# Moving 30 loads from SyncE's to GpSimd's DMA queue, new places for the input's accumulations, and other buffer counts, in an encoder layer of two sequences

## The chip, the cores and the metric

The kernel runs on one core of a Trainium2 chip. The metric is the device time in microseconds (us) of one execution. Names in the text: TensorE (PE in the profile), VectorE (DVE), ScalarE (ACT), GpSimd (POOL) and SyncE (SP). "SPq" and "POOLq" in the profile are the instruction streams of SP and GpSimd that issue transfers. Each engine works through its own instructions strictly in order; a wait at the head of one holds all that stands behind it.

## The reference

One layer of an encoder is applied to two sequences of 1024 rows and 1024 columns, each with its own conditioning vector c:

```python
def layer(x, c, ...):
    mod = jax.nn.silu(c) @ w_ada + b_ada
    sh1, sc1, ga1, sh2, sc2, ga2 = [m[:, None, :] for m in jnp.split(mod, N_MOD, axis=-1)]
    h = rmsnorm(x, g_mix) * (1.0 + sc1) + sh1
    z = h @ w_in
    q_lat, kv_lat, k_pe, f_in = ...                       # 256, 128, 64, 512 columns
    y_mla = mla_group(q_lat, kv_lat, k_pe, ...)           # attention, 4 heads, softmax over 1024 keys
    y_four = fourier_group(f_in, w_four)                  # 2-D Fourier mixing, real part
    mix = jnp.concatenate([y_mla, y_four], axis=-1) @ w_out
    x = x + ga1 * mix
    h2 = rmsnorm(x, g_ffn) * (1.0 + sc2) + sh2
    ffn = (jax.nn.silu(h2 @ w_gate) * (h2 @ w_up)) @ w_down
    return x + ga2 * ffn
```

In the attention, w_uq expands the normalised q_lat to the queries, of which 64 columns per head are rotated (rope); the keys are never expanded, since w_ukv's key part is absorbed into the queries. All arithmetic is float32; a float32 operand is split into a high part and a remainder (`split`), and a product is made of three matmuls (`mm3`, lines 83 to 85 of the profile).

## The kernel before, in words

Four stages follow each other in the profiled execution: the input projection and the Fourier transform up to about 230 us, the Fourier part's output up to about 305, the attention up to about 764, and then the feed-forward network (FFN), whose products are made by sub-block combinations with fewer multiplications (seven sums H of blocks of the normalised rows). The change concerns the third stage and its border to the fourth. Arrays named `..._d` lie in DRAM.

The attention is cut into 64 items k = 0 to 63, `items`: sequence s, block b of 256 rows, head h, half u of 128 rows. i = k % 8 is an item's place in its block. The code of the loop gives the order in which an item's work is written down, a scheduler puts each engine's instructions in order from that, and `tc.issue_after` adds constraints. What an item does:

- `scores`: TensorE makes 128 x 1024 scores (L1191 to L1200) from the absorbed queries qa and the rotated ones qp; VectorE takes the maximum mx and nb (L1206, L1207), ScalarE the exponential, VectorE 1/sum, rr, and scales p by it (L1210, L1211). SP then copies p to pr by DMA, 512 KB (`pr<-p`, L1213). pr has two buffers, so item k's copy can start once item k−2 has been transposed.
- `flip_p`, two items later: TensorE transposes pr (`ppt<-identr,pr`, L1227), ScalarE and VectorE split the result into pt; `values` multiplies pt with the latent values (`gb<-pt,ckv`) into o0b, o1b.
- the queries of the next block: `rope_q` at i = 3, 4 (through the tile hv, named qt: L847 on VectorE, L848 on GpSimd, L852 qsk), `rope_flip` at i = 5, 6 (`pqt`, L858), `absorb_q` after each odd item (qa).
- the block before: `out_step` loads its rows of the sum so far (`x<-fo_d`, L1120), adds the projection of the attention's result (`out_proj`, L1130; its bank is `gb`, of which there are two), stores them to x_d (`norm2`, L1135), normalises them (squares on ScalarE L1138, `rstd` on GpSimd L107 to L114, xn on VectorE L1143) and stores them transposed to h_d (`flip_h`, L1162).

Further work is hung on chosen items by the lists `todo[k]`:

- `add_x(i)`, 16 times: GpSimd adds a 256 x 512 part of the input x to fo_d in DRAM by an accumulating DMA (`fo_d<-in_x_dram`, L806, 512 KB). fo_d holds the Fourier part's output already.
- `gate_half` and `wv_load` (items 0 and 2 for the first sequence, 34 and 37 for the second): the gate's half is loaded into gah (one buffer, L1246), the output weights wo_d into wvr in 4 parts of 256 KB each time (L1271), and GpSimd multiplies the two (L1272).
- `comb_h` (items 49, 51, 57, 59): loads two halves of 512 KB of the first sequence's normalised rows (`hca<-h_d`, L1252), GpSimd forms sums and differences hcb of them (L140, L143), the folded combinations for the FFN, and stores 1 MB (`hc_d<-hcb`, L1262). hca and hcb have one buffer each.

At the end of the attention the FFN's first data are fetched: `prep_h` loads the first sequence's H (L1368), the first weights rgu (L1378), and `x3_load` the last block's rows (x and X, L1401). VectorE and ScalarE split H (`H<-H,H`, L63) between the last projections; GpSimd's queue holds there the x_d stores of the last blocks (L1135).

Most of the transfers named stand on SP (`nc.sync.dma_start`); those of add_x, hc_d and the last x_d stores on GpSimd (`nc.gpsimd.dma_start`).

Of the kernel before, what the change touches and what calls it, by code (L numbers as in the profile page):

```python
# [12 lines left out]
F32 = mybir.dt.float32  # L13
F32R = mybir.dt.float32r
# [7 lines left out]
P = 128  # L22
# [3 lines left out]
HEADS = 4  # L26
# [26 lines left out]
def hybrid_encoder_kernel(ctx: ExitStack, tc: tile.TileContext, a: dict):  # L53
    nc = tc.nc
# [70 lines left out]
    wo_d = dram.tile([P, 4, D], F32, name="wo_d")  # L125
# [670 lines left out]
    S = {}  # L796
# [9 lines left out]
            nc.gpsimd.dma_start(fo_d[s][bs, gs], xs[s][bs, gs], accum_op=ALU.add)  # L806

    def half(name):
        return e.tile([P, 512], F32, tag="hv", name=name, bufs=1)

    def load_seq(s, lat):
        ckv = [e.tile([P, 8, KVL], F32R, tag=f"ckv{i}", name=f"ckv{i}", bufs=1) for i in range(2)]
# [16 lines left out]
        return e.tile([P, HEADS, P], F32R, tag="qp", name="qp", bufs=4)  # L829

    def qa_tiles():
        return [e.tile([P, 256], F32R, tag=f"qa{i}", name=f"qa{i}", bufs=2) for i in range(2)]

    def rope_q(s, b, u, bankf):
        ql = S["q", s, b]
# [339 lines left out]
    with ExitStack() as st:  # L1175
# [54 lines left out]
        def values(s, b, q):  # L1230
            ckv = S[s][1]
            pts = S.pop(("pt", s, b, q))
            if q == 0:
                S["o", s, b] = [tl.tile([P, HEADS, 256], F32R, tag=f"o{i}", name=f"o{i}b{s}{b}", bufs=3) for i in range(2)]
            o = [t[:, 2 * q : 2 * q + 2, :].rearrange("p h t -> p (h t)") for t in S["o", s, b]]
            po = gbank()
            for c in range(8):
                pth, ptl = (t[:, c % 4].rearrange("p i t -> p (i t)") for t in pts[c // 4])
                mm3(po, ckv[0][:, c, :], ckv[1][:, c, :], pth, ptl, c == 0, c == 7)
            split(o[0], o[1], po)  # L1240
# [7 lines left out]
        def comb_h(s, c):  # L1248
            A = e.tile([P, 4, 512], F32, tag="lat00", name="hca")
            B = e.tile([P, 4, 512], F32, tag="lat01", name="hcb")  # L1250
            for i in range(2):
                nc.sync.dma_start(A[:, 2 * i : 2 * i + 2, :], h2_d[s][:, c + 4 * i, :].rearrange("p (a b) -> p a b", a=2))  # L1252
            a11, a21, a12, a22 = (A[:, i, :] for i in range(4))
            with tc.issue_after(here["p"]):
                add(B[:, 0, :], a21, a22, nc.gpsimd)
                sub(B[:, 2, :], a11, a21, nc.gpsimd)

            def rest():
                with tc.issue_after(here["p"]):
                    sub(B[:, 1, :], B[:, 0, :], a11, nc.gpsimd)  # L1260
                    sub(B[:, 3, :], a12, B[:, 1, :], nc.gpsimd)
                    nc.gpsimd.dma_start(hc_d[s][:, c], B)  # L1262

            S["comb"] = rest

        def wv_load(s, g):
            gs = slice(512 * g, 512 * g + 512)
            raw4 = (w if s == 0 else e).tile([P, 4, 512], F32, tag=f"lat{1 - s}{g}", name="wvr4")
            for h in range(HEADS):
                raw = raw4[:, h, :]  # L1270
                nc.sync.dma_start(raw, wo_d[:, h, gs])  # L1271
                nc.gpsimd.tensor_tensor(out=raw, in0=raw, in1=S["ga"], op=ALU.mult)  # L1272
                S["wv", h, g] = raw

# [15 lines left out]
        for c, k in enumerate((49, 51, 57, 59)):  # L1290
            todo[k].append(lambda c=c: comb_h(0, c))
            todo[k + 1].append(lambda: S.pop("comb")())
        for i, k in enumerate((6, 8, 10, 12, 17, 18, 19, 25, 26, 27, 33, 34, 35, 41, 42, 43)):
            todo[k].append(lambda i=i: add_x(i))
        for u in range(2):
            todo[60 + u].append(lambda u=u: out_load(1, 2, u))
# [45 lines left out]
    with ExitStack() as st:  # L1342
# [10 lines left out]
        def prep_h(H, s, n):  # L1353
# [3 lines left out]
            def load(i):  # L1357
                k = HK[i]
                src = h2_d[s][:, HSRC[k][0] : HSRC[k][0] + 4, 512 * HSRC[k][1] : 512 * HSRC[k][1] + 512] \
                    if isinstance(HSRC[k], tuple) else hc_d[s][:, :, HSRC[k], :]  # L1360
                if HSTAGE[s][i] is None:
                    raw[k] = [val() for _ in range(4)]
                    for c in range(4):
                        nc.sync.dma_start(raw[k][c], src[:, c, :])
                else:
                    t = quad(HSTAGE[s][i])
                    for c in (0, 2):
                        nc.sync.dma_start(t[:, c : c + 2, :], src[:, c : c + 2, :])  # L1368
                    raw[k] = t

            ahead = 4 if s == 0 else 2
# [1 line left out]
            for i in range(ahead):  # L1373
                load(i)
                if s == 0 and i == 0:
                    S["rgu"] = w.tile([P, 2, 1024], F32, tag="X0", name="rgu0", bufs=1)
                    for j in range(2):
                        nc.sync.dma_start(S["rgu"][:, j, :], a["wgu"][j, 0])  # L1378
                    x3_load()
            if s == 0:  # L1380
                yield
# [14 lines left out]
        def x3_load():  # L1396
            X1 = quad("X1").rearrange("p a b -> p (a b)")
            for u in range(2):
                xn = X1[:, D * u : D * u + D]
                x2 = tl.tile([P, D], F32, tag="o0", name="x3", bufs=3) if u == 0 else xn  # L1400
                nc.sync.dma_start(x2, fo_d[1][(6 + u) * P : (7 + u) * P, :])  # L1401
                S["x2", 1, 3, u] = x2
                S["xn", 1, 3, u] = xn

# [70 lines left out]
        for n in range(4):  # L1475
# [1 line left out]
            if n == 1:  # L1477
                norm3(0)
            if n == 2:
                fw = [tl.tile([P, 2, 512], F32R, tag=f"o{i}", name=f"fw{i}", bufs=3) for i in range(2)]  # L1480
                for i in range(2):
                    split(fw[0][:, i, :], fw[1][:, i, :], w0[i])
            prep_step((2, 0, 1, 0)[n])
# [498 lines left out]
```

## Time and profile before

| | |
|---|---|
| median of 3 runs | 2049.7 us (2049.03 to 2055.41) |
| profiled execution | 2048.47 us, span 2046.7 us |
| mean clock granted to TensorE | 0.989 |
| busy: TensorE, VectorE, ScalarE, GpSimd | 1984.9, 1425.1, 894.8, 829.5 us |
| DMA | 403.91 MB, mean 197 GB/s |
| SP's queue (q1) and GpSimd's (q0) | 344.27 MB and 57.81 MB |

A row of a timeline gives start, duration, engine, line, operation, tiles written and read, their count, and in brackets the time that the engine stood idle before, with what ended it. `x2` or `x3` behind a row means that equal instructions in succession were taken together, and its duration is then from the first one's start to the last one's end. A row of waits gives the microseconds in total, the number of waits and the longest. The duration of a DMA row is that of its issue, not of the transfer.

### The profile page before, as it was taken

How to read it: one execution, taken by the hardware profiler on the slowest of the kernel's cores; microseconds unless marked ns; L12 is line 12 of the kernel's file. 1: busy time of each engine (PE TensorE's matmuls, PEld its weight loads, DVE VectorE, ACT ScalarE, POOL GpSimd, SP SyncE). 2: the span in 40 equal slices, each digit the busy share in tenths (PEclk: the TensorE clock that was granted, in tenths of full speed). 3: DMA queues.
4: the chain of work that ended last, by engine and by line, in shares of the span. 5: the costliest groups of instructions: out<-in, count | busy, mean ns of one | idle time of the engine just before them, and what ended most of it. 6: DMA issues, size and time to landing. Idle time of an engine off the chain costs nothing.

```text
span 2046.7 us, 28591 instructions
## 1 busy us (share of the span) xinstructions
PE 1984.9 (97%) x9840; PEld 1620.8 (79%) x9840; DVE 1425.1 (70%) x2088; ACT 894.8 (44%) x1733; POOL 829.5 (41%) x1013
## 2 busy tenths in 40 slices
PE   8899998999999899999999999999999999999997
PEld 7688776788787777888888888877788888888876
DVE  5667757666677669888778676777765666667684
ACT  4565545455465455333333365453333333336441
POOL 2454122112213216888779510332664454420142
PEclk9999999999999899999999999999999999999999
DMA  9685795767675576546546587664332232258672
GB/s 377 203 292 172 253 338 180 205 175 207 207 189 189 193 285 211 200 161 221 182 152 221 170 286 251 218 235 157 125 123 103 92 114 104 94 188 279 221 232 88
DMA packets 191182, 403.91 MB, mean 197 GB/s; under 512 B 19580, under 2 KB 59260, under 8 KB 186940
## 3 DMA queue, kind: packets, MB, share of 16 engines
q1 hardware_dynamic: 172364, 344.27, 49.4%
q0 software_dynamic: 18672, 57.81, 9.5%
q8 instruction: 77, 1.26, 0.3%
q14 instruction: 69, 0.57, 0.1%
HBM read 256.46 MB, written 120.39 MB: 184 GB/s over the span
## 4 chain that ended last, share of the span: by engine, by line
PE 54%; DVE 3%; DMA 2%; POOL 1%; issue 1%; ACT 0%; SPq 0%; DVEq 0%; ACTq 0%; POOLq 0%
PE bank L84 18%; PE bank L83 18%; PE bank L85 18%; DVE wl L63 1%; DVE val L143 1%; DMA val<-x_d 0%; DMA draw<-s_d 0%; ACT wh L62 0%; POOL val L143 0%; DVE val L1779 0%; DMA rgu<-in_wgu_dram 0%; POOL rs_y L110 0%; DMA draw<-t_d 0%; DMA draw<-in_w_down_dram 0%; DVE val L140 0%
## 5 line engine op out<-in xcount | busy, mean ns | idle before, releaser
L83 PE MATMUL bank<-H,wh 128*128 128x512 f32 x1224 | 477.4, 390 | 5.6 <-DVE val L143 5.3
L85 PE MATMUL bank<-H,wl 128*128 128x512 f32 x1224 | 476.3, 389 | 0.2 <-DVE wl L63 0.2
L84 PE MATMUL bank<-H,wh 128*128 128x512 f32 x1224 | 476.2, 389 | 0.0
L143 DVE TENSOR_TENSOR val<-bank,val 128x512 f32<-128x512 f32 x244 | 166.6, 688 | 160.2 <-PE bank L85 159.0
L83 PEld LDWEIGHTS bank<-H,wh 128*128 128x128 f32 x1224 | 229.7, 188 | 57.1 <-DVE val L143 7.8
L85 PEld LDWEIGHTS bank<-H,wl 128*128 128x128 f32 x1224 | 229.7, 188 | 48.6 <-DVE wl L63 1.1
L84 PEld LDWEIGHTS bank<-H,wh 128*128 128x128 f32 x1224 | 229.8, 188 | 47.6
L63 DVE TENSOR_TENSOR wl<-draw,wh 128x512 fp32r<-128x512 f32 x286 | 201.6, 740 | 84.5 <-ACT wh L62 82.8
L62 ACT CAST wh<-draw 128x512 fp32r<-128x512 f32 x286 | 168.3, 620 | 158.3 <-PE bank L84 87.3
L84 PE MATMUL bank<-wl,wh 128*128 128x512 f32 x572 | 223.5, 391 | 2.1 <-DVE wl L63 2.1
L143 POOL TENSOR_TENSOR val<-val 128x512 f32<-128x512 f32 x58 | 84.1, 1457 | 343.0 <-DVE val L1753 189.0
L85 PE MATMUL bank<-wh,wl 128*128 128x512 f32 x572 | 222.6, 389 | 0.0
L83 PE MATMUL bank<-wh 128*128 128x512 f32 x572 | 222.6, 389 | 0.0
L62 ACT CAST wh<-rgu 128x512 fp32r<-128x512 f32 x171 | 106.3, 623 | 251.0 <-PE bank L84 192.3
L63 DVE TENSOR_TENSOR wl<-val,wh 128x512 fp32r<-128x512 f32 x133 | 145.3, 1094 | 69.5 <-ACT wh L62 69.3
L63 DVE TENSOR_TENSOR wl<-rgu,wh 128x512 fp32r<-128x512 f32 x171 | 170.2, 996 | 7.2 <-ACT wh L62 7.1
L62 ACT CAST wh<-val 128x512 fp32r<-128x512 f32 x133 | 82.3, 622 | 178.6 <-PE bank L84 160.5
L140 POOL TENSOR_TENSOR val<-rgu 128x512 f32<-128x512 f32 x80 | 113.9, 1424 | 96.5 <-DMA rgu<-in_wgu_dram 87.8
L84 PEld LDWEIGHTS bank<-wl,wh 128*128 128x128 f32 x572 | 107.3, 188 | 26.8 <-DVE wl L63 5.0
L83 PEld LDWEIGHTS bank<-wh 128*128 128x128 f32 x572 | 107.4, 188 | 22.6
L85 PEld LDWEIGHTS bank<-wh,wl 128*128 128x128 f32 x572 | 107.4, 188 | 22.2
L140 POOL TENSOR_TENSOR val<-val 128x512 f32<-128x512 f32 x89 | 119.2, 1358 | 1.3
(393 smaller groups left out, 3910.3 us busy)
## 6 DMA issues: line engine op xcount, KB each, us to landing
rgu<-in_wgu_dram SPq DMA_DIRECT2D x86, 512.0 KB
draw<-s_d SPq DMA_DIRECT2D x143, 256.0 KB
pr<-p SPq DMA_DIRECT2D x64, 512.0 KB
s_d<-val POOLq DMA_DIRECT2D x88, 256.0 KB, 3.8
draw<-t_d SPq DMA_DIRECT2D x88, 256.0 KB
s_d<-val SPq DMA_DIRECT2D x66, 256.0 KB
wada<-in_wa_dram SPq DMA_DIRECT2D x16, 1024.0 KB
draw<-in_w_down_dram SPq DMA_DIRECT2D x55, 256.0 KB
```

Source lines behind the costliest of these rows:

```text
L62: here["a"] = nc.scalar.copy(hi, src).ins
L63: here["v"] = nc.vector.tensor_tensor(out=lo, in0=src, in1=rd(hi), op=ALU.subtract).ins
L83: nc.tensor.matmul(out, lh, rh, start=first, stop=False, skip_group_check=cont)
L84: nc.tensor.matmul(out, lh, rl, start=False, stop=False, skip_group_check=cont)
L85: here["pe"] = nc.tensor.matmul(out, ll, rh, start=False, stop=last, skip_group_check=cont).ins
L140: return eng.tensor_tensor(out=out, in0=x, in1=y, op=ALU.subtract).ins
L143: return eng.tensor_tensor(out=out, in0=x, in1=y, op=ALU.add).ins
```

## The change

- All loads of wvr (16), of hca (8), the first of the first sequence's H loads (2), rgu (2) and the two of `x3_load` are issued by GpSimd instead of SP. 30 in all.
- The 16 accumulations `add_x` are hung on other items.
- The tile hv gets two buffers for one, qa three for two; the second half of the attention's result, o1 (with fw, which shares its tag), gets two for three.

```diff
     def half(name):
-        return e.tile([P, 512], F32, tag="hv", name=name, bufs=1)
+        return e.tile([P, 512], F32, tag="hv", name=name, bufs=2)
...
     def qa_tiles():
-        return [e.tile([P, 256], F32R, tag=f"qa{i}", name=f"qa{i}", bufs=2) for i in range(2)]
+        return [e.tile([P, 256], F32R, tag=f"qa{i}", name=f"qa{i}", bufs=3) for i in range(2)]
...
-                S["o", s, b] = [tl.tile([P, HEADS, 256], F32R, tag=f"o{i}", name=f"o{i}b{s}{b}", bufs=3) for i in range(2)]
+                S["o", s, b] = [tl.tile([P, HEADS, 256], F32R, tag=f"o{i}", name=f"o{i}b{s}{b}", bufs=3 - i) for i in range(2)]
...
             for i in range(2):
-                nc.sync.dma_start(A[:, 2 * i : 2 * i + 2, :], h2_d[s][:, c + 4 * i, :].rearrange("p (a b) -> p a b", a=2))
+                nc.gpsimd.dma_start(A[:, 2 * i : 2 * i + 2, :], h2_d[s][:, c + 4 * i, :].rearrange("p (a b) -> p a b", a=2))
...
                 raw = raw4[:, h, :]
-                nc.sync.dma_start(raw, wo_d[:, h, gs])
+                nc.gpsimd.dma_start(raw, wo_d[:, h, gs])
...
-        for i, k in enumerate((6, 8, 10, 12, 17, 18, 19, 25, 26, 27, 33, 34, 35, 41, 42, 43)):
+        for i, k in enumerate((6, 8, 11, 13, 16, 19, 22, 24, 26, 28, 37, 39, 41, 43, 45, 47)):
             todo[k].append(lambda i=i: add_x(i))
...
                     for c in (0, 2):
-                        nc.sync.dma_start(t[:, c : c + 2, :], src[:, c : c + 2, :])
+                        (nc.gpsimd if s == 0 and i == 0 else nc.sync).dma_start(t[:, c : c + 2, :], src[:, c : c + 2, :])
...
                     for j in range(2):
-                        nc.sync.dma_start(S["rgu"][:, j, :], a["wgu"][j, 0])
+                        nc.gpsimd.dma_start(S["rgu"][:, j, :], a["wgu"][j, 0])
...
-                nc.sync.dma_start(x2, fo_d[1][(6 + u) * P : (7 + u) * P, :])
+                nc.gpsimd.dma_start(x2, fo_d[1][(6 + u) * P : (7 + u) * P, :])
...
-                fw = [tl.tile([P, 2, 512], F32R, tag=f"o{i}", name=f"fw{i}", bufs=3) for i in range(2)]
+                fw = [tl.tile([P, 2, 512], F32R, tag=f"o{i}", name=f"fw{i}", bufs=3 - i) for i in range(2)]
```

The scheduler's order of instructions changes with it. SP issues 800 rows of transfers in place of 824, GpSimd has 884 rows in place of 866 (equal neighbours are one row). Three places matter here.

SP's queue at the beginning of the attention, items 0 to 3, with the loads of the gate (gah), of the output weights (wvr) and the copies of the probabilities (pr):

```order
 L822 DMA ql_3780<-lat_d_90 128x2x256
 L1246 DMA gah<-ga_d 128x512
-L1271 DMA wvr_3785<-wo_d 128x512 x4
-L1271 DMA wvr_3871<-wo_d 128x512 x2
-L1213 DMA pr<-p 128x1024
-L1246 DMA gah<-ga_d 128x512
-L1271 DMA wvr_3871<-wo_d 128x512
-L1213 DMA pr<-p 128x1024
-L1271 DMA wvr_3871<-wo_d 128x512
 L1213 DMA pr<-p 128x1024
 L1246 DMA gah<-ga_d 128x512
 L1213 DMA pr<-p 128x1024
+L1246 DMA gah<-ga_d 128x512
+L1213 DMA pr<-p 128x1024 x2
```

The eight wvr loads are gone from it, and the third gah load, which stood behind the copies of items 0, 1 and 2, now stands behind those of items 0 and 1, ahead of that of item 2.

SP's queue around items 50 to 53, in the second sequence, with the loads hca of `comb_h`, the x_d stores and x loads of the blocks, and pr (the first pr here is that of item 50):

```order
-L1135 DMA x_d_100<-x_6895 128x1024
-L1252 DMA hca<-h_d_104 128x1024 x2
+L1135 DMA x_d_100<-x_6889 128x1024
 L1120 DMA x_7496<-fo_d_98 128x1024
-L1213 DMA pr<-p 128x1024 x2
-L1252 DMA hca<-h_d_104 128x1024
-L1213 DMA pr<-p 128x1024
+L1213 DMA pr<-p 128x1024 x3
 L1162 DMA h_d_105<-ht 128x4x128 x2
-L1252 DMA hca<-h_d_104 128x1024
 L1213 DMA pr<-p 128x1024
```

The hca loads are gone from between the x_d stores and the copies of probabilities; the same happens a block later, around item 58.

GpSimd's queue at the end of the attention, from the last store of combinations to the norm of the rows that follow; x and X are the last block's rows, H and rgu the FFN's first data:

```order
 L1262 DMA hc_d_87<-hcb 128x2048
+L1401 DMA x_8375<-fo_d_98 128x1024
 L1135 DMA x_d_100<-x_8075 128x1024
+L1368 DMA H_8368<-h_d_104 128x2x512 x2
+L1378 DMA rgu_8371<-in_wgu_dram 128x1024 x2
+L1401 DMA X_8374<-fo_d_98 128x1024
 L107 TENSOR_SCALAR rs_v<-ms_8276 128x1
 L110 TENSOR_TENSOR rs_y<-rs_v,mhalf 128x1
```

The H, rgu and X loads, five transfers, now stand behind the x_d store and ahead of the norm's first operation L107.

## The prediction

> **What bounds the kernel now.** I read the page first, then the waits of TensorE by what ended them.
>
> ```profile
> PE 1984.9 (97%) x9840; PEld 1620.8 (79%) x9840; DVE 1425.1 (70%) x2088; ACT 894.8 (44%) x1733; POOL 829.5 (41%) x1013
> PE ppt L1227 <- DMA pr<-p: 19.3, 7, 6.8
> PE pqt L858 <- DVE qsk L852: 2.2, 1, 2.2
> PE gb L83 <- DVE qt L847: 1.2, 1, 1.2
> PE ps_s L1191 <- ACT qa L62: 1.1, 1, 1.1
> PE ps_s L1193 <- DVE qa L63: 0.8, 1, 0.8
> ```
>
> TensorE is busy 97% of the span, so a faster transfer pays only where TensorE stands still. The wait rows give total, times and longest: 19.3 us in seven waits of the transposes for a copy of probabilities (pr), and four single waits in the preparation of the queries. All that the change can win lies in these rows and in what follows a stall. So next I looked at the places: TensorE's timeline (start, duration, in brackets the idle time before), and windows around them (busy time of five engines, then the granted clock, DMA share, GB/s).
>
> ```profile
> 379.75 0.85 PE L1227 MATMUL ppt<-identr,pr 128*128 128x128 f32 x8 [1.44 <-DMA pr<-p]
> 541.79 0.98 PE L1227 MATMUL ppt<-identr,pr 128*128 128x128 f32 x6 [3.67 <-DMA pr<-p]
> 652.62 0.85 PE L1227 MATMUL ppt<-identr,pr 128*128 128x128 f32 x8 [3.16 <-DMA pr<-p]
> 709.85 0.97 PE L1227 MATMUL ppt<-identr,pr 128*128 128x128 f32 x6 [6.81 <-DMA pr<-p]
> 538.00:545.10 7.10, 3.43 (x16) 2.87 (x15) 2.74 (x8) 2.47 (x5) 0.72 (x1) 0.76 0.64 162
> 649.40:657.70 8.30, 5.14 (x25) 4.44 (x25) 4.66 (x10) 3.92 (x9) 6.18 (x6) 0.79 0.33 135
> 703.00:715.80 12.80, 5.99 (x26) 5.12 (x25) 3.64 (x7) 3.45 (x8) 5.88 (x5) 0.60 0.62 252
> 716.00:720.00 4.00, 2.39 (x18) 1.74 (x16) 2.38 (x5) 3.83 (x10) 0.00 (x0) 1.00 0.99 349
> ```
>
> The three long stalls are followed by work at a granted clock that brings their windows to 0.76, 0.79 and 0.60; the last window, around the short qa waits, keeps 1.00. A stall of over 3 us thus costs its length and some work at half clock, one of about 1 us its length alone. The Trainium skill ("TensorE: Matmul & The Clock Gate", Part 1) has the array throttled to half after an idle window of about 3.4 us; by that rule the 3.16 us might have left the clock alone and the gain at 652 would be 3.2. The row says 0.79, and the row decides.
>
> **The gains.** What made pr late at the three places:
>
> ```profile
> 533.25 0.88 POOL L806 DMA_DIRECT2D fo_d<-in_x_dram  x1
> 528.69 5.61 SPq L1213 DMA_DIRECT2D pr<-p  x2
> 640.38 0.81 SPq L1252 DMA_DIRECT2D hca<-h_d  x2
> 641.84 3.75 SPq L1213 DMA_DIRECT2D pr<-p  x2
> 640.65 0.69 POOL L1262 DMA_DIRECT2D hc_d<-hcb  x1 [0.30 <-POOL hcb L140]
> 698.33 0.81 SPq L1252 DMA_DIRECT2D hca<-h_d  x2
> 699.78 4.00 SPq L1213 DMA_DIRECT2D pr<-p  x2
> ```
>
> - Place 541: an accumulation of the input (L806) runs beside the pr of item 34. Slots 33, 34, 35 become 37, 39, 41, so it is gone from here: 3.67, and at half clock (1 − 0.76) × 7.10 = 1.70, together 5.4 at most. I take 5.0.
> - Place 652: the pr of item 50 stands on SP behind two hca loads (L1252), which there wait for GpSimd, and it travels beside them and beside the hc_d store of 640.65. With hca on GpSimd, behind that store, pr leaves up to 641.84 − 640.38 = 1.46 us sooner, and the megabyte of hca is no longer ahead of it: at most 3.16 + (1 − 0.79) × 8.30 = 4.9. I take 4.0.
> - Place 709: the same with item 58, 699.78 − 698.33 = 1.45 us sooner. At most 6.81 plus half of the window's 5.99 busy us, 9.8. I take 8.5, since the next pr may then be the late one.
> - Place 379: slot 10 becomes 11, 1.4 at most. Slots 6 and 8 stay, and what they cost stays.
> - Buffers: a second hv and a third qa can take the four short waits, 2.2 + 1.2 + 1.1 + 0.8 = 5.3 at most, and nothing where TensorE waits for VectorE's or ScalarE's work itself and not for a buffer. With place 379 I take 4.7 of 6.7. Two buffers for o1 cost nothing in the items, where a block's result is read out by the projection before the block after the next begins to write. At the end, fw (the FFN's first split weights) takes the buffer that block (1,2) leaves, so its split moves behind that block's last projection; the FFN wants it only after the last block's projection, which covers it: zero.
>
> Gains: 5.0 + 4.0 + 8.5 + 4.7 = 22.2 us, with ends of 8.5 (place 709 alone) and 26.8.
>
> **The costs.** The opening, items 0 to 3:
>
> ```profile
> 319.14 5.52 POOL L1272 TENSOR_TENSOR wvr<-wvr,gah 128x512 f32<-128x512 f32 x4 [3.20 <-DMA gah<-ga_d]
> 319.42 0.47 SPq L1213 DMA_DIRECT2D pr<-p  x1
> 324.69 0.33 SPq L1246 DMA_DIRECT2D gah<-ga_d  x1
> 329.75 1.10 PE L1227 MATMUL ppt<-identr,pr 128*128 128x128 f32 x8 [1.59 <-DVE mx L1206]
> ```
>
> The gah load of 324.69 waits until the products L1272 have read its one buffer, 319.14 + 5.52 = 324.66. The pr of 319.42 stood ahead of it and now stands behind it, and leaves at about 325.0, that is 5.6 us later. Between the two, TensorE has other work, and 1.59 us of its time at 329.75 are idle anyway: I take 2.0, with ends of 0 and 5.6.
>
> New slots for L806: 39 and 47 are last items of a block of eight, whose pr has the least time.
>
> ```profile
> 480.16 0.89 POOL L806 DMA_DIRECT2D fo_d<-in_x_dram  x1
> 480.74 7.89 SPq L1213 DMA_DIRECT2D pr<-p  x2
> DMA  8644349936049999899999998421004999989989
> 566.88 0.47 SPq L1213 DMA_DIRECT2D pr<-p  x1
> 573.72 0.79 PE L1227 MATMUL ppt<-identr,pr 128*128 128x128 f32 x8
> ```
>
> The digits are the DMA engines' busy tenths in slices of 0.30 us from 480.10. Beside an accumulation the traffic ends with the 28th, at 488.5, 7.8 us after pr's issue. At a last item (the pr of 566.88) TensorE is ready 573.72 − 566.88 = 6.8 us after the issue. So each of the two stalls 1.0, with a trace of half clock 1.5: 3.0 in all, with ends of 0 and 8 (two stalls of three quarters of that at 541).
>
> The tail, with the H, rgu and X loads of the next stage:
>
> ```profile
> 735.88 1.45 SPq L1368 DMA_DIRECT2D H<-h_d  x2
> 739.10 0.53 POOL L1135 DMA_DIRECT2D x_d<-x  x1 [24.78 <-DVE x L1130]
> fo_d<-in_x_dram POOLq DMA_DIRECT2D x16, 512.0 KB, 8.7
> 741.63 2.54 DVE L63 TENSOR_TENSOR H<-H,H 128x1024 fp32r<-128x1024 f32 x2 [0.39 <-ACT H L62]
> 744.08 0.68 DVE L1130 TENSOR_TENSOR x<-x,gb 128x512 f32<-128x512 f32 x1
> 747.05 0.39 PE L83 MATMUL gb<-wv,o0b 128*128 128x512 f32 x1
> 756.37 0.75 DVE L1143 TENSOR_SCALAR xn<-x,rs_r 128x1024 f32<-128x1024 f32 x1 [1.55 <-POOL rs_r L114]
> ```
>
> On SP these loads left from 735.88. On GpSimd they stand behind the x_d store, which waits for VectorE and goes at 739.10, so H leaves at about 739.7. By the median landing of GpSimd's own 512 KB accumulations, 8.7 us, it is there at 748.4. VectorE splits H (0.39 for ScalarE's cast, 2.54) ahead of the sum L1130 in its order, and that sum frees the bank which TensorE fills from 747.05. L1130 then ends at 748.4 + 0.4 + 2.5 + 0.7 = 752.0: TensorE stands 5.0 us. Half clock after it, and the last norm, whose rstd on GpSimd now follows five issues (1.55 us at 756.37 already), add 2 by estimate. I take 7. If H needs only 4 us to land, L1130 ends at 747.3 and nothing much is left; the high end is 12, with rgu late by the same 5 for the sums behind.
>
> The other moved loads are 16 of wvr and eight of hca. Their first reader is GpSimd itself, in order, and SP is spared them.
>
> ```profile
> POOL 2454122112213216888779510332664454420142
> ```
>
> In the attention items (the 7th to 15th slice of 51.2 us) GpSimd is busy one to three tenths. 24 issues at 0.9 (the row of L806) are 22 us spread over 430; that fits into its idle time, so zero, unless the third rival holds.
>
> Costs: 2.0 + 3.0 + 7.0 = 12.0, with ends of 0 and 25.6. Sum: 12.0 − 22.2 = −10.2, say −10. Against the profiled execution's 2048.47 that is 2038.5; the median of the runs, 2049.7, lies 1.2 above it, so the median comes to about 2039.5.
>
> **The rivals.**
> 1. The covers hold: tail and new slots cost nothing, the opening 2. −22.2 + 2 = −20.2, which is 2029.5. For it: H leaves only 739.7 − 735.9 = 3.8 us later, and TensorE's bank is due at 747.05. Against it: the 8.7 us of the GpSimd queue.
> 2. The costs are full: tail 12, slots 8, opening 2, against 22.2: 2049.5, no change. For it: SP's next H loads fill its queue in the same microseconds, and at 480 a transfer beside another one took more than its own time. Against it: both ends at once.
> 3. Slower. GpSimd becomes what others wait for. The rstd of a norm (L107 to L114) and the rope sum L848 stand behind loads that themselves wait for a buffer or a store, and VectorE, in order, waits in its L1143 with the maxima and p scalings of the items behind it.
>
> ```profile
> DVE xn L1143 <- POOL rs_r L114: 6.8, 4, 3.5
> ```
>
> One such wait is already 3.5 us long. The second sequence has eight norms; if five of them wait 3.5 us, and p and its pr come late with them, that is 17.5 more, −10 + 17.5 = 7.5, 2057. It makes the change slower from 16 us of such waits on. Against it: 6.8 us in four waits now.
> 4. Loads from GpSimd starve. VectorE scales p once per item:
>
> ```profile
> 566.06 0.75 DVE L1211 TENSOR_SCALAR p<-p,rr 128x1024 f32<-128x1024 f32 x1
> ```
>
> If GpSimd cannot send a load on while such an operation runs, each of the six tail loads comes up to 0.75 later, in a row 4.5: −10 + 4.5 = −5.5, 2044. The Trainium skill states this rule ("SBUF — State Buffer", SBUF: two separate sides): while VectorE is in a two-port mode, GpSimd cannot write descriptors, and it advises a queue of SP or ScalarE, which speaks against this change. The slow landings of L806 here would fit it, but a full ring explains them as well.
>
> **How the numbers follow.** My sum 0.42, by itself 2033 to 2046; rival 1 0.17; rival 2 0.18; rival 3 0.11; rival 4 0.12. A measurement of this kernel can tell about 0.3%, 6.1 us, from no change: faster is below 2043.6, slower above 2055.8. Faster: 0.33 of my 0.42, all of rival 1, 0.04 of rival 4, together 0.54. Slower: rival 3, 0.11. Same: the remaining 0.35. The range leaves out rival 3 and half of rival 1: 2030 to 2053.
>
> **What would show it.** Right: no transpose waiting over 1 us at 541, 652 and 709, and the clock near 1.0 there; the pr of item 2 leaving at 324 to 326; small waits of L1227 after items 39 and 47; the first H landing near 748, and TensorE standing at 747. Wrong: H there by 744 (rival 1); VectorE's waits for GpSimd above 15 us (rival 3); or the pr of item 58 still late behind the hc_d store.

## The result: 0.46% slower

The changed kernel's median is 2058.7 us (18 runs, 2054.48 to 2064.37), that of the kernel before 2049.14 (18 runs, 2044.15 to 2055.41). The ratio is 1.0046, 95% interval 1.0035 to 1.0056, some 9.4 us. The forecast was 2039.5, with a range of 2030 to 2053. Runs of one kernel lie up to 14 us apart (experiment 1: 2046.46 to 2060.21), so below medians and ratios to before decide, and a profile, which is that of one run, only shows where.

TensorE's waits in the changed kernel, as those shown of before:

```profile
PE ppt L1227 <- DMA pr<-p: 16.9, 10, 3.1
PE gb L83 <- DVE x L1130: 6.3, 1, 6.3
PE ps_s L1191 <- ACT qa L62: 3.4, 2, 2.6
PE pht L1157 <- DVE pt L63: 3.0, 1, 3.0
```

The longest wait for pr is 3.1 us in place of 6.8, but there are ten for seven, and the three rows below it are waits that before did not have at this length. To see where, I cut both profiles at the same work: from the first scores to VectorE's maximum (L1206) of items 8, 32, 40, 48, 56 and 63, and on to the end of the last projection. The windows of before, then of the changed kernel, without that of items 8 to 32 (busy times, granted clock, DMA share, GB/s):

```profile
305.23:347.94 42.71, 39.15 (x209) 29.81 (x208) 32.52 (x63) 22.28 (x43) 14.49 (x14) 0.96 0.64 207
509.24:567.50 58.26, 54.59 (x301) 43.89 (x302) 37.87 (x68) 29.35 (x64) 17.64 (x28) 0.97 0.65 199
567.50:620.58 53.08, 53.08 (x301) 42.66 (x302) 41.17 (x77) 33.52 (x72) 8.10 (x20) 1.00 0.72 198
620.58:678.53 57.95, 54.79 (x301) 44.05 (x302) 39.67 (x68) 29.45 (x64) 17.07 (x24) 0.97 0.56 200
678.53:731.18 52.65, 44.23 (x225) 34.91 (x226) 30.59 (x50) 22.43 (x47) 14.02 (x16) 0.90 0.53 186
731.18:764.56 33.38, 31.66 (x161) 25.92 (x160) 24.83 (x34) 22.44 (x35) 7.76 (x21) 1.00 0.89 322
```

```profile
302.30:354.71 52.41, 41.91 (x209) 31.83 (x208) 32.45 (x63) 22.23 (x43) 18.59 (x22) 0.87 0.57 181
517.33:571.85 54.52, 53.35 (x301) 42.69 (x302) 36.22 (x68) 29.52 (x64) 18.93 (x29) 1.00 0.64 201
571.85:626.73 54.88, 53.24 (x300) 42.58 (x300) 41.16 (x76) 33.56 (x72) 10.79 (x24) 1.00 0.76 201
626.73:686.67 59.94, 54.75 (x301) 44.30 (x302) 39.19 (x69) 29.54 (x64) 19.39 (x28) 0.97 0.64 203
686.67:732.07 45.40, 43.33 (x225) 33.81 (x226) 31.00 (x50) 22.24 (x47) 15.41 (x19) 0.96 0.62 216
732.07:773.51 41.44, 35.01 (x161) 27.88 (x160) 25.48 (x34) 22.32 (x35) 10.82 (x26) 0.88 0.75 268
```

TensorE does the same work in each (its counts agree within one), so a difference in length is waiting or clock:

| stretch | before | changed | difference |
|---|---|---|---|
| up to the first scores | 305.23 | 302.30 | −2.9 |
| opening, to item 8 | 42.71 | 52.41 | +9.7 |
| items 8 to 32 | 161.30 | 162.62 | +1.3 |
| items 32 to 40 (place 541) | 58.26 | 54.52 | −3.7 |
| items 40 to 48 | 53.08 | 54.88 | +1.8 |
| items 48 to 56 (place 652) | 57.95 | 59.94 | +2.0 |
| items 56 to 63 (place 709) | 52.65 | 45.40 | −7.2 |
| tail | 33.38 | 41.44 | +8.1 |
| behind it (to the spans 2046.7 and 2056.8) | | | +1.1 |

The sum is +10.1. The opening alone takes back nearly all that places 541 and 709 win; of its 9.7 us, 6.9 are more idle time of TensorE and 2.8 the same matmuls at a lower clock (busy 41.91 in place of 39.15).

How far can stretches of one profile each be trusted? The other kernels' profiles give ranges. The opening takes 40.8 to 43.2 us with the loads on SP and the old buffer counts (before and experiments 6, 7, 11, 13, 18; 8, whose accumulations fall into it, is left out), 45.0 to 46.3 with the loads on SP and the new counts (1, 3, 16, 17), 48.7 and 51.2 with the loads on GpSimd and the old counts (5, 12), and 50.3 to 52.9 with both (the changed kernel, 2, 9, 15). So some 3 of the 9.7 come with the buffers, which also let the attention start some 3 sooner, and by the means 6 to 8 with the loads. Place 541 is less sure: with the old places its stretch takes 55.0 to 58.5 us, with the new ones, or those of 13, 53.0 to 55.2, and the profile of before had the longest wait for pr there of the five with the old places (3.67 us against 2.0 to 2.8). Items 56 to 63 take 52.3 to 57.1 with hca on SP and 43.9 to 49.0 with hca on GpSimd.

**The opening.** First rope's sum in GpSimd's timeline before, then SP's, GpSimd's and TensorE's of the changed kernel:

```profile
315.21 0.73 POOL L848 TENSOR_TENSOR qt<-qt 128x256 f32<-128x256 f32 x1
316.51 0.33 SPq L1246 DMA_DIRECT2D gah<-ga_d  x1
316.95 0.49 SPq L1213 DMA_DIRECT2D pr<-p  x1
326.18 0.33 SPq L1246 DMA_DIRECT2D gah<-ga_d  x1
326.68 1.64 SPq L1213 DMA_DIRECT2D pr<-p  x2
307.46 2.57 POOL L1271 DMA_DIRECT2D wvr<-wo_d  x4 [3.58 <-PE ps_s L1194]
316.42 1.67 POOL L1271 DMA_DIRECT2D wvr<-wo_d  x3
318.11 1.21 POOL L848 TENSOR_TENSOR qt<-qt 128x256 f32<-128x256 f32 x1
321.20 4.95 POOL L1272 TENSOR_TENSOR wvr<-wvr,gah 128x512 f32<-128x512 f32 x4 [1.88 <-DMA gah<-ga_d]
320.08 0.57 PE L1191 MATMUL ps_s<-lat,qa 128*128 128x512 f32 x1 [2.61 <-ACT qa L62]
324.15 1.23 PE L1227 MATMUL ppt<-identr,pr 128*128 128x128 f32 x8 [3.07 <-DMA pr<-p]
331.14 1.23 PE L1227 MATMUL ppt<-identr,pr 128*128 128x128 f32 x8 [2.75 <-DMA pr<-p]
```

Two holds work together. On SP, the gah loads of 316.51 and 326.18 wait for GpSimd's products, with the pr of items 1 and 2 (316.95, 326.68) behind them: waits of 3.07 and 2.75 us. On GpSimd, the first four loads leave 5.2 us after the first scores (on SP, before, 0.1 us after them, at 305.36), so the products start 8.5 us after them in place of 4.6; and the three loads of 316.42 (1.67 us to issue) stand ahead of rope's sum L848. That sum starts 15.8 us after the first scores, in place of 10.0; ScalarE's qsk and, behind it, qa are late, and TensorE waits 2.61 us for qa. Three waits inside 14 us bring the stretch's clock to 0.87 (0.96 before).

**Place 652.** The wait for the pr of item 50 is gone, and the 3.0 us wait of the transposes of xn stands in its place. Two rows of GpSimd's timeline before, then GpSimd's and ScalarE's of the changed kernel:

```profile
651.14 1.26 POOL L143 TENSOR_TENSOR hcb<-hca 128x512 f32<-128x512 f32 x1 [7.16 <-DMA hc_d<-hcb]
653.60 0.73 POOL L848 TENSOR_TENSOR qt<-qt 128x256 f32<-128x256 f32 x1
649.81 1.08 POOL L1252 DMA_DIRECT2D hca<-h_d  x2
659.27 1.29 POOL L143 TENSOR_TENSOR hcb<-hca 128x512 f32<-128x512 f32 x1 [6.86 <-DMA hca<-h_d]
662.21 0.72 POOL L848 TENSOR_TENSOR qt<-qt 128x256 f32<-128x256 f32 x1
662.96 0.40 ACT L851 CAST qsk<-qt 128x256 fp32r<-128x256 f32 x1 [3.05 <-POOL qt L848]
```

GpSimd waits 6.86 us for hca, which it asked for itself only behind its last store. Rope's sum stands behind two of the combinations, ScalarE waits 3.05 us for it, VectorE's qsk and pt follow, and TensorE's transposes want a bank that pt empties. But the change did not make this hold. Before, GpSimd waited 7.16 us at the same place (there, by the row, for its store hc_d), and rope's sum stood behind the same combinations, 33.0 us after the start of this stretch in place of 35.5, of which TensorE's wait at item 47 makes 1.76. What was new is that TensorE no longer came late itself: by these rows, its 3.16 us wait for pr had covered the other. In experiment 7, where only the hca loads move, rope's sum starts at 653.51, no later than the 653.60 of before, and TensorE waits 3.11 us for the transposes of xn all the same.

**The tail, and three short waits.**

```profile
739.96 0.54 POOL L1135 DMA_DIRECT2D x_d<-x  x1 [19.22 <-DVE x L1130]
740.49 1.47 POOL L1368 DMA_DIRECT2D H<-h_d  x2
750.57 1.23 DVE L63 TENSOR_TENSOR H<-H,H 128x1024 fp32r<-128x1024 f32 x1 [8.39 <-ACT H L62]
754.47 0.79 PE L83 MATMUL gb<-wv,o0b 128*128 128x512 f32 x1 [6.32 <-DVE x L1130]
579.83 0.86 PE L1227 MATMUL ppt<-identr,pr 128*128 128x128 f32 x8 [1.61 <-DMA pr<-p]
635.16 0.86 PE L1227 MATMUL ppt<-identr,pr 128*128 128x128 f32 x8 [1.76 <-DMA pr<-p]
716.71 1.12 PE L1227 MATMUL ppt<-identr,pr 128*128 128x128 f32 x8 [1.19 <-DMA pr<-p]
```

The first four rows are the chain that was forecast: x_d, H behind it at 740.49 (it landed 9.6 us later in the median of its two loads), VectorE's split at 750.57, TensorE's wait of 6.32. The last three are the waits after items 39 and 47 and the next late pr, that of item 59.

### The profile page after: what moved, and what is told of

It is laid out like the page before. It is cut to its first block, busy times and chain, and to the rows that moved or that the text cites. A ratio compares the mean times of both kernels' runs of the same rounds, so it can differ in the third digit from the quotient of the medians.

```text
span 2056.8 us, 28578 instructions
## 1 busy us (share of the span) xinstructions
PE 1988.1 (97%) x9840; PEld 1621.8 (79%) x9840; DVE 1424.7 (69%) x2088; ACT 894.8 (44%) x1733; POOL 846.8 (41%) x1043
## 4 chain that ended last, share of the span: by engine, by line
PE 51%; DVE 4%; DMA 2%; issue 1%; POOL 1%; ACT 1%; SPq 0%; DVEq 0%; ACTq 0%; POOLq 0%
PE bank L83 17%; PE bank L84 17%; PE bank L85 17%; DVE wl L63 2%; DMA draw<-s_d 1%; DVE val L143 1%; ACT wh L62 1%; DMA draw<-t_d 1%; POOL val L143 1%; DMA draw<-in_w_down_dram 0%; DMA val<-x_d 0%; DMA rgu<-in_wgu_dram 0%; POOL rs_y L110 0%; DVE val L1779 0%; DVE val L1753 0%
## 5 line engine op out<-in xcount | busy, mean ns | idle before, releaser
L85 PEld LDWEIGHTS bank<-H,wl 128*128 128x128 f32 x1224 | 229.8, 188 | 48.7 <-DVE wl L63 1.1
L63 DVE TENSOR_TENSOR wl<-val,wh 128x512 fp32r<-128x512 f32 x133 | 149.9, 1129 | 71.2 <-ACT wh L62 71.0
```

Of the source, the lines that this page charges most:

```text
L63: here["v"] = nc.vector.tensor_tensor(out=lo, in0=src, in1=rd(hi), op=ALU.subtract).ins
L85: here["pe"] = nc.tensor.matmul(out, ll, rh, start=False, stop=last, skip_group_check=cont).ins
```

## The experiments

Each median is compared with runs of the kernel before on the same chip; "ratio" is to these. Variants that ran on different chips are compared by their ratios.

**1. The opening's loads back on SP.** In the changed kernel:

```diff
-                nc.gpsimd.dma_start(raw, wo_d[:, h, gs])
+                (nc.sync if s == 0 else nc.gpsimd).dma_start(raw, wo_d[:, h, gs])
```

> The changed kernel, with the first sequence's eight wvr loads back on SP. Theory (the opening is what was mis-sized: between the maxima of items 3 and 5 the changed kernel lost 10.5 us against before, by three stalls of 2.61, 3.07 and 2.75 us and two stretches at half clock): about 10 us under the changed kernel, 2048 to 2049 in the median, the three stalls gone, pr of item 2 leaving SP near 316 to 320. Rival (the opening is late because of something that stays, such as the accumulations at items 6 and 8 or the buffer counts): within 3 us of the changed kernel.

Median 2054.6 (12 runs), ratio 1.0023 (1.0009 to 1.0036). The stretch:

```profile
303.57:348.91 45.34, 39.34 (x209) 29.90 (x208) 32.45 (x63) 22.17 (x43) 14.21 (x14) 0.96 0.66 210
```

45.3 us in place of 52.4: 7 of the 9.7 come back there. In the time it is 4 to 5; the theory's 10 was missed, and intervals as wide as these do not tell 5 from 7. Of the three stalls, the one for qa is gone; waits for pr of 2.42 and 1.17 us remain.

**2. The tail's loads back on SP** (first H, rgu, x, X: `nc.sync` as before, the rest of the change kept).

> The changed kernel, with the loads of the first H, rgu, x and X back on SP. Theory (the tail costs what the prediction gave it): about 7 us under the changed kernel, 2051 to 2052; the 6.32 us stall of TensorE at 748 gone, the first H there by 742. Rival (the stall is made up for in the feed-forward part, whose first weights wait anyway): within 2 us of the changed kernel although the stall is gone.

Median 2049.46 (12 runs), ratio 1.0001 (0.9990 to 1.0012): 9 us under the changed kernel. The tail's stretch is 33.4 again. The theory holds, with 9 us for its 7.

**3. Both back on SP.**

> The changed kernel with both sets back on SP; the hca loads, the second sequence's wvr, the new places of the accumulations and the buffer counts stay. Theory (opening and tail are separate and add up): 17 us under the changed kernel, about 2042, that is 7 to 8 under before. Rival (the gains at 541, 652 and 709 are worth less than the profile's stalls say, or are lost again in the second half): 2046 or more, no faster than before.

Median 2048.61 (12 runs), ratio 0.9989 (0.9976 to 1.0002). The theory's 2042 was missed; it is the rival's number. Beside experiment 2, the opening's loads are worth only 1 to 3 us here, with overlapping intervals. What stays of the change is not told from nothing, so a gain in it is eaten by something else in it: in this profile items 48 to 56 take 63.50 us in place of 57.95, with a wait of 3.68 at the transposes of xn. Experiments 6, 7 and 13 to 16 look for the rest.

**4. The gate loads gah on GpSimd as well.** In the changed kernel:

```diff
-            nc.sync.dma_start(S["ga"], ...)
+            nc.gpsimd.dma_start(S["ga"], ...)
```

> The changed kernel, with the four gate loads gah on GpSimd as well, so that no load on SP waits for GpSimd's products any more. Theory A (the opening is lost on SP: the copies pr of items 1 and 2 stand behind gah loads that wait for L1272): pr of item 1 leaves near 313.9 and that of item 2 near 319, the stalls of 3.07 and 2.75 us go with their half clock, the qa stall stays: about 7 us under the changed kernel, 2051 to 2052. Theory B (it is lost on GpSimd: rope's sum L848 and the products stand behind the issues of the loads): no gain, the changed kernel within 2 us, with the qa stall longer.

Median 2057.66 (7 runs), ratio 1.0038 (1.0024 to 1.0051): not told apart from the changed kernel in time, which is theory B's forecast. In its profile, that of the fastest of its runs, the opening takes 46.99 us in place of 52.41, which speaks for A as the larger part; the wait for qa stays, with 2.9 us. Inconclusive, so it was repeated in the old kernel (12 and 14).

**5. The opening's loads alone**, in the kernel before (only the first sequence's wvr on GpSimd).

> The kernel before, with only the first sequence's eight wvr loads moved to GpSimd. Theory (this one move makes the opening longer, by SP's gah loads that wait for L1272 ahead of pr, and by GpSimd's own queue): 7 to 10 us over before, 2057 to 2060; from the first scores to the maximum of item 8 some 52 us in place of 42.7. Rival (the opening is only late together with the second hv buffer, which lets the attention start 2 us sooner into the Fourier part's stores): at most 4 over before.

Median 2062.64 (6 runs) against 2050.49, ratio 1.0051 (1.0034 to 1.0068). By itself this move costs 10 to 12 us (7 to 14 by the interval), as much as the whole change loses. It needs no second buffer and no new places for that: the rival falls.

```profile
305.90:354.55 48.65, 40.73 (x209) 30.91 (x208) 34.64 (x62) 22.07 (x43) 18.30 (x22) 0.89 0.57 179
```

The theory's 52 us for the opening was missed: the stretch is 5.9 longer than before (8.5 in experiment 12, whose pr of item 2 is held in the same way). The rest of this profile's 14 us lies elsewhere: 3.0 in items 8 to 32, 4.4 in items 56 to 63 by the clock alone (last section), 3.0 behind the tail, less 2.8 at place 541. That all of the 10 to 12 us is lost in the opening is not shown.

**6. The accumulations' new places alone**, in the kernel before.

> The kernel before, with only the new places of the accumulations. Theory (541 wins 4, the last items 39 and 47 lose 1.8 each): within 2 us of before; waits of L1227 for pr of items 39 and 47 of 1 to 2 us each. Rival (the prediction's balance of the same terms, 6.4 to 3): 3 us under before.

Median 2049.51 (12 runs), ratio 0.9997 (0.9986 to 1.0008). No change in time, as the theory has it. Its profile, which is that of the fastest of the 12 runs, does not show why: items 32 to 40 take 53.03 us in place of 58.26, items 40 to 56 together 112.87 in place of 111.03, and there is no wait over 1 us for the pr of items 39 and 47. So 5.2 us are won and 1.8 lost in the profile, and what takes the rest back in the time stays open.

**7. The hca loads alone on GpSimd**, in the kernel before.

> The kernel before, with only the eight hca loads moved to GpSimd. Theory (the stalls of the transposes at 652 and 709 go, about 13 us, but the combinations then wait on GpSimd for hca to land, rope's sum L848 stands behind them, and TensorE waits 3 to 4 us at its transposes of xn, with half clock): 5 to 8 us under before, 2042 to 2045. Rival (the prediction's, no new wait): 12 us under, 2038. Rival (GpSimd's queue gives it all back): within 2 us of before.

Median 2043.13 (8 runs) against 2050.49, ratio 0.9956 (0.9941 to 0.9971): 7 to 9 us faster, the part of the change that pays. Its waits of TensorE from 620 to 730 us:

```profile
PE pht L1157 <- DVE pt L63: 3.1, 1, 3.1
PE ppt L1227 <- DMA pr<-p: 1.2, 1, 1.2
```

Both long waits for pr are gone, and the one at the transposes of xn is there without the rest of the change. The gain is place 709's, 45.86 us in place of 52.65; items 48 to 56 take 58.75 in place of 57.95. The theory's time was met.

**8. Opening and tail on SP, and the accumulations where pr had time to spare.** Experiment 3 with items 4, 5, 12, 16, 17, 20, 24, 25, 28, 36, 40, 41, 44, 45, 48, 52.

> The third experiment's kernel (opening and tail loads on SP), with the accumulations at items 4, 5, 12, 16, 17, 20, 24, 25, 28, 36, 40, 41, 44, 45, 48, 52, whose pr had 4 us and more to spare. Theory (an accumulation costs time only where the pr beside it has less than some 5.5 us to spare): no wait for pr over 1 us after item 4, 6 to 8 us under the third experiment, about 2041. Rival (GpSimd's queue or the ring makes another wait of them): within 2 us of the third experiment.

Median 2050.41 (12 runs), ratio 0.9996 (0.9983 to 1.0009). The theory fell:

```profile
356.86 1.22 PE L1227 MATMUL ppt<-identr,pr 128*128 128x128 f32 x8 [5.70 <-DMA pr<-p]
```

With the accumulations done early, the x loads that wait for them leave SP early too, at 345.9 and 346.3, and with a load of latents (L814, 346.8) they now stand ahead of the pr of item 6 (348.37; in experiment 3, 341.25), for which TensorE waits 5.70 us. The spare time of one pr says nothing on what the earlier transfer releases.

**9. The x_d store ahead of the tail's loads moved to SP**, in the changed kernel.

> The changed kernel, with the x_d store that stands ahead of the H loads on GpSimd moved to SP. Theory (the tail is lost because the loads stand behind the store's wait and then behind SP's full queue): the first H leaves before 737 on the changed kernel's clock of events, is there 4 to 5 us later, the stall of 6.3 us goes: 6 to 8 us under the changed kernel, about 2051. Rival (the loads cannot leave sooner, because their buffers come free then, and land slowly for the traffic beside them): the stall stays at 4 us or more, less than 3 us gained.

Median 2055.25 (12 runs), ratio 1.0025 (1.0015 to 1.0035): about 4 us under the changed kernel, half of what the theory expected. The first rows are GpSimd's and SP's, the last the tail's window:

```profile
722.46 1.47 POOL L1368 DMA_DIRECT2D H<-h_d  x2
744.45 0.34 SPq L1135 DMA_DIRECT2D x_d<-x  x1
745.10 1.03 SPq L1368 DMA_DIRECT2D H<-hc_d  x2
736.80:773.59 36.79, 33.60 (x161) 27.06 (x160) 25.37 (x34) 22.14 (x35) 7.87 (x20) 0.95 0.67 236
```

H now leaves at 722.46, 18 us sooner: its buffers were free, and x_d was what held it. The tail shrinks from 41.4 to 36.8 us, and TensorE's wait from 6.3 to 2.0; it does not come to 33.4, for x_d now holds SP's own H loads (745.10; 737 in the changed kernel). A store that waits for the last sum holds the queue that it is in.

**12 and 14. The opening's two holds apart.** Experiment 5, with gah on GpSimd too: in 12 for the first sequence only, in 14 all four.

> The fifth experiment's kernel (before, with the first sequence's wvr loads on GpSimd), with the first sequence's gate loads gah on GpSimd too. Theory A (about half of the 10 to 12 us is lost on SP, where pr of items 1 and 2 stand behind gah loads that wait for L1272; the rest on GpSimd): 4 to 6 us under the fifth, 2056 to 2058; pr of item 2 leaves within 0.2 us of its p. Theory B (all of it is lost on GpSimd): within 2 us of the fifth.

Median 2058.58 (5 runs), ratio 1.0050 (1.0035 to 1.0065), as experiment 5: a miss, because the third gah load, ahead of the pr of item 2, is the second sequence's and had stayed on SP: it left at 331.44, and pr behind it at 331.94, 9.7 us after its p was done.

> The fifth experiment's kernel (before, with the first sequence's wvr loads on GpSimd), with all four gate loads gah on GpSimd too; the ninth experiment had left the third one, which is the second sequence's, ahead of pr of item 2. Theory A (SP's share of the opening's loss is the two copies held by gah): pr of items 1 and 2 leave at once, and from the first scores to the maximum of item 8 some 46 us in place of 48.6 to 51; the median 4 to 6 us under the fifth's. Theory B (GpSimd's queue, and the loads beside pr, make up nearly all of it): pr leaves at once, but the stretch stays at 48 us or more, the median within 3 us of the fifth's.

Median 2056.56 (12 runs) against 2050.82, ratio 1.0027 (1.0014 to 1.0040), about 5 us under experiment 5 (the intervals overlap). What the expectation calls the ninth experiment is 12 here. SP's queue, and the stretch:

```profile
313.77 16.11 SPq L1213 DMA_DIRECT2D pr<-p  x4
306.30:352.13 45.83, 40.06 (x209) 30.02 (x208) 33.95 (x62) 22.38 (x43) 19.43 (x24) 0.93 0.58 190
```

No gah stands between the four pr. This is theory A's number: the opening's stretch loses 3.1 us here, against 5.9 and 8.5 with gah on SP (5 and 12), so about half of its loss is SP's, and the rest GpSimd's (the wait for qa stays at 1.45 us, that for the pr of item 1 at 2.3).

**13 and 11. The best kernel.** The kernel before with hca on GpSimd and the accumulations at 6, 8, 11, 13, 16, 19, 22, 24, 26, 28, 36, 37, 40, 41, 43, 44 (13), and then:

```diff
-        for c, k in enumerate((49, 51, 57, 59)):
+        for c, k in enumerate((49, 53, 57, 61)):
```

> The kernel before with the hca loads on GpSimd (the seventh experiment) and the accumulations at items 6, 8, 11, 13, 16, 19, 22, 24, 26, 28, 36, 37, 40, 41, 43, 44, that is the change's places without the last items 39, 45 and 47. Theory (the two effects lie in different items and add: 7 from hca, 5 from place 541): about 2039 to 2041, no wait for pr over 1 us between items 30 and 50. Rival (the accumulations' half of it is worth no more than in the sixth experiment): 2042 to 2044.

Median 2041.66 (8 runs), ratio 0.9966 (0.9952 to 0.9979). Beside experiment 7 (0.9956) the new places show no gain; it is nearer to the rival's number. In its profile, that of the slowest of its runs, items 32 to 40 win 5.5 us against experiment 7, and items 40 to 48, with the accumulations of 40, 41, 43 and 44, lose 4.9.

> The previous kernel, with the combinations at items 49, 53, 57, 61 in place of 49, 51, 57, 59, so that rope's sums L848 of items 51 and 52 stand ahead of the combinations that wait for hca in GpSimd's queue. Theory (the wait of some 3 us at TensorE's transposes of xn near 655 comes from L848 behind these combinations): that wait goes, 3 to 4 us under the previous kernel. Rival (it comes from something else, such as the norm): the wait stays and the time is the same.

Median 2034.77 (5 runs) against 2049.35, ratio 0.9935 (0.9921 to 0.9948): 6 us under 13, 13 under before. GpSimd's rope sums, and the window of items 48 to 56:

```profile
642.50 0.73 POOL L848 TENSOR_TENSOR qt<-qt 128x256 f32<-128x256 f32 x1 [0.81 <-DVE qt L847]
650.00 0.74 POOL L848 TENSOR_TENSOR qt<-qt 128x256 f32<-128x256 f32 x1 [6.77 <-DVE qt L847]
619.83:672.92 53.09, 53.09 (x301) 42.65 (x302) 39.95 (x69) 29.39 (x64) 19.93 (x28) 1.00 0.60 204
```

Both sums wait only for VectorE, and TensorE is busy all of the 53.09 us. The wait of 3 us (3.88 in the profile of 13) was L848 behind the combinations. The 6 us are more than the theory's 3 to 4; 5.2 of them show in this window (58.29 in 13), so the place 652 pays only now.

**15. The same two items in the changed kernel.**

> The changed kernel, with the combinations at items 49, 53, 57, 61. Theory (the gain expected at 652 was given back by rope's sum L848, which waits in GpSimd's queue behind combinations that wait for hca): the 3.0 us stall at the transposes of xn near 665 goes, and the items 48 to 56 take 53 to 56 us in place of 59.9; the median 4 to 6 us under the changed kernel, 2053 to 2055. Rival (only together with the other changes of the eleventh kernel): less than 2 us.

Median 2054.95 (12 runs), ratio 1.0018 (1.0004 to 1.0033): 4 to 6 us under the changed kernel; items 48 to 56 take 57.20 us in place of 59.94, and the 2.3 us wait of item 47 is all that is left there. The theory holds but for the stretch, where it had at most 56.

**16, 17, 18. Buffers and the second sequence's wvr.** The best kernel with both of them (and the opening and tail on SP), with the buffer counts alone, and with these eight loads on GpSimd alone.

> The changed kernel, with the opening's and the tail's loads on SP, the combinations at items 49, 53, 57, 61, and the accumulations at 6, 8, 11, 13, 16, 19, 22, 24, 26, 28, 36, 37, 40, 41, 43, 44: the best kernel so far (the combinations' experiment) plus the change's buffer counts and the second sequence's wvr loads on GpSimd. Theory (these two parts are worth 0 to 3 us): 2032 to 2036, within 3 us of that kernel. Rival (the attention that starts 2 us sooner runs into the Fourier part's stores, and GpSimd has more to issue): 2038 to 2042.

> The best kernel (before with hca on GpSimd, the combinations at 49, 53, 57, 61 and the accumulations without 39, 45 and 47), with only the change's buffer counts (hv 2, qa 3, o1 2) added. Theory (the buffers bring the attention's start forward by 2 to 3 us, and the first items lose that again, since the Fourier part's stores are still on their way): the first scores 2 us sooner, the stretch to the maximum of item 8 some 3 us longer; the median within 3 us of the best kernel. Rival (the buffers are the whole difference of the sixteenth kernel): 4 to 7 us over the best kernel. Rival (the prediction's 3 to 5 us of gain): 2031 or less.

> The best kernel, with only the second sequence's eight wvr loads on GpSimd. Theory (they have time, items 34 to 40, and cost nothing): within 2 us of the best kernel. Rival (they hold rstd and rope's sum there as in the opening): 3 to 6 us over it.

Medians 2041.16, 2039.96 and 2038.93 (6 runs each), ratios 0.9948 (0.9929 to 0.9967), 0.9945 (0.9923 to 0.9967), 0.9948 (0.9929 to 0.9966). None is better than the best kernel, and the intervals overlap its own: neither part shows a gain. By the ratios each loses 2 to 3 us, by the bare medians 4 to 6 as the rivals of all three have it; which of the two it is stays open. The buffers' profile:

```profile
301.14:347.46 46.32, 39.93 (x209) 29.92 (x208) 32.76 (x62) 22.37 (x43) 14.05 (x14) 0.93 0.60 205
```

The first scores come 2.6 us sooner than in the best kernel (303.77), the stretch to item 8 takes 4.0 us longer (42.30 there).

## Why the prediction was wrong

By its own steps, with the stretches of the two profiles:

- **The opening, "I take 2.0, with ends of 0 and 5.6": failed.** The one late pr that the step priced came as described: that of item 2 left at 326.68, and TensorE waited 2.75 us for it. Left out were two more waits, 2.61 us for qa and 3.07 for the pr of item 1, and the lower clock behind three waits. They come from GpSimd: in order, it issues the loads between the products and ahead of rope's sum (the price of issuing was set to zero over 430 us of idle time, where it was not idle), so that rope's sum, the products, and with them gah and pr, are later still. GpSimd's new order, which I had followed only at the tail, shows the loads between the products and ahead of L848. The stretch measured 9.7, of which 6 to 8 are the loads' and some 3 the buffers'. In the time the size is less sure: 10 to 12 alone (experiment 5), 1 to 5 when taken back out of the changed kernel (1, and 3 against 2).
- **Place 652, "I take 4.0": failed.** pr came in time as forecast. But the step looked only at the wait that ended last. Rope's sum, behind combinations that wait 7 us on GpSimd, was as late before and hidden behind the wait for pr; without that, TensorE waits for it instead. The stretch became 2.0 longer, 1.8 of it item 47's. Experiments 11 and 15 get the gain by moving the combinations.
- **Buffers and place 379, "4.7 of 6.7": failed, about 0.** Of the four short waits only the 2.2 us for qsk is gone. The 1.2 for qt is there twice, also with two buffers of hv, so it was not for a buffer. The wait at place 379 is 1.90 in place of 1.44. The attention starts 2.9 sooner and the first items lose it again (experiment 17).
- **Place 541 (5.0) and 709 (8.5): right in kind,** 3.7 and 7.2, with the next pr late by 1.2 as foreseen. At 541 the 3.67 us wait on which the 5.0 was built was a long one, as the other profiles show.
- **The new slots (3.0): right in this profile,** 1.61 and 1.76 us of waits at items 39 and 47 and 3.6 by the stretches. Experiment 6 has the new places without these waits, and no gain in time.
- **The tail (7.0): right,** 8.1 by the stretch, 9 by experiment 2, by the chain described.

By terms, of the 20 us between the forecast sum and the profiles' difference, 11 lie ahead of item 32 (opening, buffers and place 379), 4 at place 652, and about 1 each at 541, 709, the slots, the tail and behind it.

- **Rival 3** (GpSimd as what others wait for) came nearest, at 0.11 far too low. That its 2057 lies near the measured 2058.7 is luck, for its path was wrong: not rstd, for which VectorE waits 9.1 us in five waits in place of 6.8 in four (its sign was over 15), but rope's sum, SP's gah and, at the tail, x_d.
- **Rivals 1 and 2** fell: the tail was not covered (6.32 us of waiting), and tail and slots cost 8.1 and 3.6, not 12 and 8.
- **Rival 4** is no cause of the tail's loss: none of its six loads is issued beside a p scaling, and VectorE stands idle for 8.39 us while H is on its way. Three of the 16 wvr loads are issued mainly beside one; they take 0.73 to 0.95 us to issue, the others 0.54 to 0.68, and land no later (3.4 to 5.1 us after the issue, the others 3.2 to 7.0). The Trainium skill's rule ("SBUF — State Buffer", SBUF: two separate sides) is not needed for any of the waits above, though the longer issues would fit it, and no run here excludes it.

## What to carry to other kernels

An in-order queue that mostly idles is not free: price a moved load by what stands behind it at that place, its issue and its wait apart, and follow also the waits on other queues that end with that engine's work. When a move takes away a wait, look at what else is due at that place: a second chain that ends just as late takes over, as rope's sum did at 652; here two items' other places were worth 6 us more on top of the same move. And test a bundle in parts: here the hca loads paid 7 to 9 us, the tail's loads lost 9, and the opening's lost 1 to 12, depending on the kernel around them.

## What the runs showed of the hardware

A wait of TensorE does not have one price. The same wait for the pr of item 58, in two kernels that do not change it (experiments 5 and 6, the windows of items 56 to 63, and the wait in each):

```profile
685.20:742.28 57.08, 48.91 (x225) 37.78 (x226) 30.60 (x51) 22.43 (x47) 13.74 (x16) 0.82 0.49 172
PE ppt L1227 <- DMA pr<-p: 6.6, 1, 6.6
672.50:725.00 52.50, 43.77 (x225) 34.39 (x226) 30.70 (x50) 22.34 (x47) 13.72 (x16) 0.93 0.53 187
PE ppt L1227 <- DMA pr<-p: 7.1, 1, 7.1
```

The stretch with the shorter wait is 4.6 us longer, all of it clock: 0.82 against 0.93, with the same matmuls busy for 48.91 us in place of 43.77. The Trainium skill ("TensorE: Matmul & The Clock Gate", Part 1) has the gate watch a window that runs free of the kernel, so that the number of slow matmuls differs from run to run; these rows agree, and may be part of why runs of one kernel lie up to 14 us apart, which was not tried.
